# Mixture-of-experts handover: routing order, first group's places, a store's queue and the hold on expert loads

## Chip, cores and metric

The kernel runs on one core of one Trainium2 chip. The metric is device microseconds of one execution; lower is better. All inputs lie in HBM, the output is written to HBM.

## What is computed

One encoder layer over 1024 tokens of width 1024: latent attention and a two-way gated recurrence, a cross attention, and then a two-level mixture of experts. The change touches the last part and the handover into it:

```python
def hier_moe(h, w_group, b_group, w_expert, b_expert, w_gate, w_up, w_down):
    ...
    g_sel = jnp.argmax(g_logits, axis=-1)                      # one of 8 groups per token
    g_weight = jnp.take_along_axis(g_prob, g_sel[:, None], axis=-1)
    e_logits = jnp.take_along_axis(e_logits, g_sel[:, None, None], axis=1)[:, 0]
    top_logit, top_local = lax.top_k(e_logits, MOE_TOP_K)      # two of the group's 8 experts
    top_w = jax.nn.softmax(top_logit, axis=-1) * g_weight
    ...
    hb = jax.nn.silu(xb @ w_gate[e]) * (xb @ w_up[e])          # per expert, hidden width 256
    return hb @ w_down[e]
```

The result is the residual stream plus the two weighted expert outputs of each token. Each of the 64 experts has three matrices of 1 MB in float32, so 192 MB of weights are read once.

## The kernel before

**The part ahead of the change.** `cross_out(t)` (L1126 to L1157) computes the last 128 rows of tile t of the residual stream into `xt`, stores them to the scratch tensor `x3_d` (L1148) and to `out` (L1149), both on SyncE's DMA queue, and takes the mean square of each row. `logits(t)` (L1263 to L1274) turns the rows over, multiplies by the router's weights and writes 72 logits per row to `L`. This runs for t = 0 to 7; tile 7 is the last.

**Routing.** `route_groups` (L1276) handles tiles 0 to 4 early, beside the matmuls of `cross_out`, and tiles 5 to 7 at the end. It picks the group of each row, counts with triangular matmuls (`behind`) how many rows of the same group stand ahead of it, and places row numbers in `idf` by one-hot matmuls (L1334). `idx0` (L1338) holds the row numbers of group 0, in two windows of 96 rows. The inner function `route_experts` (L1340) picks two experts per row, computes weights, and the place of each row in its expert's list, into `meta`; L1377 stores it to the scratch tensor `meta_d` on ScalarE's queue.

**Handover.** `gather` (L1408) fetches a group's rows from `x3_d` into `xg0` and `xg1` by indirect DMAs on GpSimd's queue, `gather_meta` (L1418) the matching rows of `meta_d` into `mt0` and `mt1`. For group 0 both are gathered right after routing. 48 matmuls without use (L1436) run in between. The gathered `mt` also releases `idx` (L1438, the row numbers of the other groups) and, by a one-element copy on GpSimd (L1444, L1445), the loads of expert 4; the rows gathered for group 1 release those of expert 5 in the same way. Then `cnt`, `lim` and `nro` count the overflow rounds.

**Experts.** `moe` (L1602) runs 32 pairs of experts, 4 pairs per group, under an order written out by hand for TensorE, VectorE and ScalarE. For group 0 it first makes the one-hot places `gm` from `mt` (L1478), splits the rows into a high and a low part (`hi` on ScalarE, L137; `lo` on VectorE, L138), spreads them by one-hot matmuls (L1519, L1520) into `xT`, and makes the slot weights (L1498). Then per pair: `up` (L1542), `scatter` of the pair before (L1580), `turn_hidden`, a piece of the next `spread`, `down` (L1566). Gate and up matrices have 6 buffers and down matrices 4, so the loads of experts 6 and 7 are issued (L1446, L1447 on SyncE's queue) when `up` of the first pair has read experts 0 and 1, and so on; the loads of experts 4 and 5 are the last that need no expert's buffer back.

**Pools.** SBUF space is a stack. The pools `e2`, `e1` (which holds `xt`) and `ew` (which holds the cross attention's output weights) are closed before `wp2` (experts 3 to 5) and then `mx` (`xg`, `mt`) are opened on their space; `mp` (`gm`, `hi`, `lo`, `xT`) reaches over the space of the routing pool `rp`. Outside the parts with an order by hand, a scheduler orders each engine's and queue's instructions by when it takes them to be ready.

## Time and profile before

| | us |
|---|---|
| median of 3 runs | 1623.76 |
| lowest and highest of them | 1619.84, 1625.01 |
| the profiled execution's own time | 1627.78 |
| its span, first to last instruction | 1625.9 |
| PE busy | 1536.2 |
| DVE busy | 811.5 |
| ACT busy | 671.0 |
| POOL busy | 369.9 |

PE is TensorE's matmuls, PEld its weight loads, DVE VectorE, ACT ScalarE, POOL GpSimd, SP SyncE; a name with a q behind it is the engine's own sequencer or DMA issue. Times are microseconds from the span's start. A row of a timeline gives the start, the duration, the engine, the line and operation, what is written and read, the count of merged instructions, and in square brackets the idle time of the engine just before and what it waited for. The granted clock is a share of TensorE's full speed: 1.00 is 2.4 GHz and 0.50 is 1.2 GHz.

### The profile page before, as it was taken

Reading aid. Unit: us, or ns where it says so; the run is one execution under the profiler, and the core shown is the slowest. Engines: PE = TensorE matmul, PEld = TensorE weight load, DVE = VectorE, ACT = ScalarE, POOL = GpSimd, SP = SyncE. Lnnn points to the kernel's source line nnn. Section 1 sums busy time; section 2 is a strip of 40 time slices with the busy share of each in tenths; the row PEclk is TensorE's granted clock in tenths of the full one; section 3 lists DMA queues with packets and bytes.
Section 4 is the critical chain, followed back from the end, with each engine's and each line's share of the span. In section 5 each row is a group of like instructions: output and inputs, shape, how many; then the busy total and the mean of one; then the engine's idle time right before and its main releaser. Section 6 shows DMA issues by size and latency. Waiting matters only on the chain.

```text
span 1625.9 us, 25727 instructions
## 1 busy us (share of the span) xinstructions
PE 1536.2 (94%) x9956; PEld 1175.0 (72%) x9956; DVE 811.5 (50%) x1501; ACT 671.0 (41%) x1290; POOL 369.9 (23%) x497
## 2 busy tenths in 40 slices
PE   6999999998989999999999999988999999999995
PEld 6999977877878888888899988875444545444541
DVE  6177267677748777775624342253343332332321
ACT  5255234545647776664445552113232221222210
POOL 3087100000216765443122112013010110000000
PEclk9999999999999999999999999999999999999998
DMA  8144312204544553424633258978999999999992
GB/s 266 35 151 183 111 40 53 79 20 143 177 154 124 163 167 91 126 69 136 218 117 102 75 203 281 329 266 324 422 405 423 402 399 424 404 403 423 424 424 78
DMA packets 170830, 359.10 MB, mean 221 GB/s; under 512 B 31440, under 2 KB 118156, under 8 KB 146124
## 3 DMA queue, kind: packets, MB, share of 16 engines
q1 hardware_dynamic: 163504, 342.89, 57.2%
q0 software_dynamic: 4608, 14.33, 2.6%
q8 instruction: 81, 1.33, 0.3%
q10 hardware_dynamic: 2588, 0.16, 0.1%
q14 instruction: 49, 0.40, 0.1%
HBM read 296.92 MB, written 60.41 MB: 220 GB/s over the span
## 4 chain that ended last, share of the span: by engine, by line
PE 54%; issue 31%; DMA 6%; POOL 3%; DVE 3%; ACT 2%; SPq 0%; POOLq 0%; ACTq 0%; DVEq 0%
PE big L519 8%; PE sm L130 6%; PE big L1142 5%; PE sm L986 5%; PE big L167 4%; PE big L464 4%; PE big L895 3%; PE sm L895 2%; DMA out_dram<-xg,idx 2%; PE sm L553 2%; PE sm L241 2%; PE sm L738 2%; PE sm L739 2%; PE sm L826 1%; PE big L1059 1%
## 5 line engine op out<-in xcount | busy, mean ns | idle before, releaser
L1542 PE MATMUL pm<-wgu,xT 128*64 128x512 f32 x1024 | 232.3, 592 | 0.0
L1542 PEld LDWEIGHTS pm<-wgu,xT 128*64 128x64 f32 x1024 | 79.5, 137 | 142.1 <-issue 138.1
L1566 PE MATMUL pm<-wd,hT 128*64 128x512 f32 x512 | 129.8, 615 | 9.5 <-DMA wd<-in_moe_w_down_dram 7.4
L141 DVE SCALAR_TENSOR_TENSOR yl<-pm,ws,yh 128x512 fp32r<-128x512 f32 x64 | 48.0, 751 | 114.3 <-ACT yh L140 114.3
L1590 POOL DMA_INDIRECT out_dram<-xg,idx x16 | 15.1, 946 | 382.2 <-DVE xg L1588 379.8
L1566 PEld LDWEIGHTS pm<-wd,hT 128*64 128x64 f32 x512 | 37.9, 140 | 76.7 <-issue 53.5
L138 DVE TENSOR_TENSOR ptl<-sm,pth 128x512 fp32r<-128x512 f32 x128 | 84.2, 682 | 17.5 <-ACT pth L137 17.0
L137 ACT ACTIVATE pth<-sm 128x512 fp32r<-128x512 f32 x128 | 73.3, 595 | 44.0 <-PE sm L130 43.1
L140 ACT ACTIVATE yh<-pm,ws 128x512 fp32r<-128x512 f32 x64 | 44.0, 687 | 110.6 <-PE pm L1566 109.6
L725 DVE TENSOR_REDUCE st<-big 128x1 f32<-128x1024 f32 x64 | 77.9, 1217 | 15.7 <-PE big L167 12.7
L130 PE MATMUL sm<-ident,pr 128*128 128x128 f32 x576 | 83.5, 273 | 1.1 <-DVE xt L910 0.4
L1545 ACT ACTIVATE sg<-pm,ws 128x256 f32<-128x256 f32 x32 | 15.2, 475 | 167.5 <-PE pm L1542 167.5
L1546 DVE SCALAR_TENSOR_TENSOR sg<-pm,ws,sg 128x256 f32<-128x256 f32 x32 | 15.5, 484 | 129.9 <-ACT sg L1545 127.7
L130 PEld LDWEIGHTS sm<-ident,pr 128*128 128x128 f32 x576 | 68.7, 141 | 11.8 <-POOL pr L729 0.7
L727 ACT ACTIVATE pr<-big,st 128x1024 f32<-128x1024 f32 x64 | 71.4, 1116 | 11.3 <-DVE st L725 11.0
L729 POOL TENSOR_SCALAR pr<-pr,st 128x1024 f32<-128x1024 f32 x64 | 72.1, 1127 | 5.5
L1522 ACT ACTIVATE xT<-pm,wcol 128x256 f32<-128x256 f32 x64 | 30.4, 474 | 98.9 <-PE pm L1520 98.4
L738 PE MATMUL sm<-pth,mv 128*128 128x256 f32 x256 | 65.4, 292 | 3.9 <-DVE ptl L138 3.2
L1519 PE MATMUL pm<-gm,hi 96*128 96x256 f32 x256 | 66.4, 297 | 2.7 <-ACT hi L137 2.7
L1520 PE MATMUL pm<-gm,lo 96*128 96x256 f32 x256 | 63.9, 286 | 1.6 <-DVE lo L138 1.6
L739 PE MATMUL sm<-ptl,mv 128*128 128x256 f32 x256 | 63.4, 285 | 0.0
L154 ACT ACTIVATE whi<-raw 128x1024 fp32r<-128x1024 f32 (+1 forms) x52 | 47.4, 925 | 30.6 <-DMA raw<-in_x_w_kv_dram 13.2
(452 smaller groups left out, 3782.3 us busy)
## 6 DMA issues: line engine op xcount, KB each, us to landing
wgu<-in_moe_w_gate_dram SPq DMA_DIRECT2D x64, 1024.0 KB
wgu<-in_moe_w_up_dram SPq DMA_DIRECT2D x64, 1024.0 KB, 20.3
wd<-in_moe_w_down_dram SPq DMA_DIRECT2D x64, 1024.0 KB, 20.1
x_d<-xt SPq DMA_DIRECT2D x24, 512.0 KB, 5.0
raw<-in_w_in_dram SPq DMA_DIRECT2D x20, 512.0 KB, 3.7
xt<-in_x_dram SPq DMA_DIRECT2D x16, 512.0 KB, 5.8
raw<-in_x_w_kv_dram SPq DMA_DIRECT2D x16, 512.0 KB, 5.9
xt<-x_d SPq DMA_DIRECT2D x16, 512.0 KB, 4.1
```

What stands on the lines that cost most here:

```text
L130: te.transpose(out=out_, in_=in_, identity=ident[0:in_.shape[0], 0:in_.shape[0]])
L137: s.activation(hi, ps, AF.Copy)
L138: v.tensor_tensor(lo, ps, hi.bitcast(F32), op=ALU.subtract)
L519: te.matmul(ps[:, n0:n0 + 512], lhsT=l_[:, k], rhs=r_[:, k, n0:n0 + 512], start=(k == 0 and i == 0), stop=(k == KD - 1 and i == 2))
L725: v.tensor_reduce(st[:, 1:2], sp, op=ALU.max, axis=AX.X, negate=True)
L738: te.matmul(ov, lhsT=vt[:, kt], rhs=pth[:, kt], start=(kt == 0), stop=False)
L739: te.matmul(ov, lhsT=vt[:, kt], rhs=ptl[:, kt], start=False, stop=(kt == NT - 1))
L895: te.matmul(ps[:, n * 512:n * 512 + 512], lhsT=l_[:, k], rhs=r_[:, half * K2 + k, n0:n0 + 512], start=(k == 0 and i == 0), stop=(k == K2 - ...
L986: te.matmul(ps[:, j], lhsT=l_[:, k, t * P:(t + 1) * P], rhs=r_[:, k], start=(i == 0 and k == 0), stop=(i == 2 and k == KD - 1))
L1142: te.matmul(ps[:, n0:n0 + 512], lhsT=l_, rhs=r_[:, k, n0:n0 + 512], start=(k == 0 and i == 0), stop=(k == KD - 1 and i == 2))
L1542: te.matmul(ps[64 * e:64 * e + 64], lhsT=st_["xT"][q // 2][:, k, c0:c0 + CAP], rhs=we[e][:, :, k], start=(k == 0), stop=(k == KD - 1))
L1566: te.matmul(ps[64 * e:64 * e + 64], lhsT=hT[:, c, 64 * e:64 * e + 64], rhs=we[e][:, c, ns], start=(c == 0), stop=(c == 1))
```

## The change

- The last tile's store to `x3_d` moves from SyncE's to ScalarE's queue; its store to `out` stays on SyncE's.
- From the last `logits` to the handover, TensorE and VectorE follow the order of the program text, so all of `route_groups` (up to `idx0`) comes before `route_experts`.
- The places of group 0 (`mt0`, in the long-lived pool `rt`) come from a one-hot matmul at the end of `route_experts`, one part for tiles 0 to 4 and one for tiles 5 to 7; the gather of `meta_d` for group 0 is gone. `idx` is a plain copy.
- Matmuls without use stand at six places: 8, 12, 16 and 10 within the routing and 16 behind it, each 288 columns wide, in place of 48 at once.
- Expert 4's loads wait for nothing but their buffer; expert 5's wait for group 0's second window of rows.
- The counting of the rounds moves into pair 3 of `moe`.
- For group 0, `gm` is made for 4 experts, then rows and spread one half after the other, then `gm` for the other 4 experts, the row weights and the slot weights.
- The zero rows `zr` are a quarter as wide and stored by a repeated read.

```diff
-        nc.sync.dma_start(x3_d[ts, :], xt)
+        (nc.scalar if t == NT - 1 else nc.sync).dma_start(x3_d[ts, :], xt)
         nc.sync.dma_start(out[ts, :], xt)
...
+    def warm(n):
+        ps = sm(288)
+        for _ in range(n):
+            te.matmul(ps, lhsT=ones, rhs=still, start=True, stop=True)
...
+            slf, sel, mr = r8("slf", GP), r8("sel", 2), r8("mr", 2, 17)
+            v.tensor_copy(slf, sl)
+            v.tensor_tensor(sel, hoh[:, :, 0:2], og[:, :, 0:1].to_broadcast([P, n, 2]), op=ALU.mult)
+            for c0, c1, src in ((0, 8, rk), (8, 17, mt[:, :, 8:17])):
+                v.tensor_tensor(mr[:, :, :, c0:c1], src[:, :, None, :].to_broadcast([P, n, 2, c1 - c0]),
+                                sel[:, :, :, None].to_broadcast([P, n, 2, c1 - c0]), op=ALU.mult)
+            if last:
+                warm(10)
+            ps = sm(34, GP)
+            for t in range(n):
+                te.matmul(ps, lhsT=slf[:, t], rhs=mr[:, t].rearrange("p w c -> p (w c)"), start=(t == 0), stop=(t == n - 1))
...
+                v.tensor_tensor(mt0[:, :, 0:17], ps, mpart, op=ALU.add)
+                v.tensor_scalar(mt0[:, :, 0:8], mt0[:, :, 0:8], -1.0, None, op0=ALU.add)
...
+    order = ExitStack()
+    order.enter_context(tc.manual_schedule(engines={mybir.EngineType.PE, mybir.EngineType.DVE}))
     logits(NT - 1)
...
-    for _ in range(4):
-        warm = sm(288)
-        for _ in range(12):
-            te.matmul(warm[0:GP], lhsT=sl[:, 0], rhs=sl.rearrange("p t c -> p (t c)"), start=True, stop=True)
-    gather_meta(mx, ahead[0])
-    v.tensor_scalar(idx, idf[:, :, 0:2], ahead[0][1][1][:, 23:24], None, op0=ALU.add)
+    warm(16)
+    order.close()
+    for w in range(2):
+        ahead[0][w][1] = mt0[:, w]
+    v.tensor_copy(idx, idf[:, :, 0:2])
...
-    load_gu(4, ahead[0][1][1][:, 16:17])
+    load_gu(4)
+    load_gu(5, ahead[0][1][0][:, 0:1])
     ahead.append(gather(mx, idx_of(1)))
     gather_meta(mx, ahead[1])
-    load_gu(5, ahead[1][0][0][:, 0:1])
...
-        prep_places(mp, ahead.pop(0), slot0, st0)
-        prep_rows(mp, st0, 0)
-        prep_rows(mp, st0, 1)
+        first = ahead.pop(0)
+        one_hot(mp, first, slot0, st0, 0, 4)
         for kh in range(2):
+            prep_rows(mp, st0, kh)
             for _ in spread(mp, pm, st0, 0, kh):
                 pass
+        one_hot(mp, first, slot0, st0, 4, 8)
+        row_weights(mp, first, st0)
         slot_weights(mp, pm, st0)
```

## Rows read from the trace of the kernel before

**Rows 1.** The page's list of 40 equal slices of the span (40.6 us each): the mean busy share of the 16 DMA engines, in tenths.

```profile
DMA  8144312204544553424633258978999999999992
```

**Rows 2.** Busy time by stretch around and after the handover. Columns: the stretch and its length, then busy us (and instructions) of PE, PEld, DVE, ACT, POOL, the granted clock, the DMA engines' busy share and GB/s.

```profile
1078.00:1091.00 13.00, 7.18 (x70) 6.42 (x69) 9.27 (x59) 3.25 (x7) 0.55 (x1) 0.85 0.96 328
1091.00:1095.00 4.00, 4.00 (x23) 3.56 (x22) 1.59 (x10) 0.00 (x0) 1.68 (x2) 0.64 0.13 19
1095.00:1099.00 4.00, 3.14 (x26) 2.86 (x24) 0.00 (x0) 0.77 (x1) 2.44 (x3) 1.00 0.65 194
...
1113.00:1116.00 3.00, 3.00 (x18) 1.00 (x16) 0.00 (x0) 0.00 (x0) 1.61 (x4) 1.00 0.22 33
1116.00:1126.00 10.00, 10.00 (x60) 5.10 (x58) 3.28 (x6) 3.56 (x7) 0.00 (x0) 1.00 0.97 401
1126.00:1226.00 100.00, 100.00 (x524) 48.90 (x522) 37.37 (x72) 27.22 (x43) 8.27 (x8) 1.00 1.01 415
...
1526.00:1590.00 64.00, 62.11 (x306) 29.71 (x306) 18.65 (x34) 13.57 (x23) 1.86 (x2) 1.00 1.01 421
```

**Rows 3.** Who waited for whom from 1080 us on: on SyncE's DMA queue first, then on TensorE. Columns: the waiting engine and line, what it waited for, us in total, times, longest us.

```profile
SPq L1446 <- DMA wd<-in_moe_w_down_dram: 45.2, 22, 2.6
...
PEld pm L1566 <- DMA wd<-in_moe_w_down_dram: 13.1, 8, 3.4
```

**Rows 4.** Timeline of SyncE's DMA issues around the handover: expert 3's three loads, the last tile's two stores, then the loads of experts 5 and 6.

```profile
1077.89 0.33 SPq L1198 DMA_DIRECT2D wgu<-in_moe_w_gate_dram  x1
...
1078.75 0.42 SPq L1198 DMA_DIRECT2D wd<-in_moe_w_down_dram  x1
1079.27 0.60 SPq L1148 DMA_DIRECT2D x_d<-xt  x1
1079.91 0.45 SPq L1149 DMA_DIRECT2D out_dram<-xt  x1
...
1114.83 0.33 SPq L1446 DMA_DIRECT2D wgu<-in_moe_w_gate_dram  x1
...
1117.00 0.33 SPq L1446 DMA_DIRECT2D wgu<-in_moe_w_gate_dram  x1
```

**Rows 5.** Timeline of the handover, all engines: the last logits, the row numbers of group 0, the places, the gathers, the split of the rows, the spread, the slot weights and the first `up`.

```profile
1083.08 0.29 DVE L1274 SCALAR_TENSOR_TENSOR L<-sm,meta,bb 128x72 f32<-128x72 f32 x1 [2.24 <-PE sm L1273]
...
1089.98 0.16 DVE L1338 CAST idx<-idf 96x2 int32<-96x2 f32 x1
...
1090.39 7.75 PE L1436 MATMUL sm<-sl 128*96 128x288 bf16 x48
...
1092.01 0.18 DVE L1376 TENSOR_SCALAR meta<-rk 128x24 f32<-128x24 f32 x1
...
1092.26 0.37 ACTq L1377 DMA_DIRECT2D meta_d<-meta  x1
...
1093.01 1.15 POOL L1414 DMA_INDIRECT xg<-x_d,idx  x1 [11.78 <-DVE nro L1469]
...
1098.23 4.24 ACT L137 ACTIVATE hi<-xg 96x512 fp32r<-96x512 f32 x4 [9.72 <-PE sm L1436]
1099.64 0.24 DVE L1438 TENSOR_SCALAR idx<-idf,mt 96x16 int32<-96x16 f32 x1 [6.98 <-DMA mt<-meta_d,idx]
...
1101.72 4.10 DVE L138 TENSOR_TENSOR lo<-xg,hi 96x512 fp32r<-96x512 f32 x4
...
1109.00 0.95 PE L1498 MATMUL pm<-wh,gm 96*128 96x18 f32 x8
...
1109.89 2.37 PE L1542 MATMUL pm<-wgu,xT 128*64 128x512 f32 x10
```

**Rows 6.** Timeline of VectorE in the routing: two instructions of which the second needs the first, then two of which the second does not need the one just before.

```profile
1083.41 0.18 DVE L1289 TENSOR_REDUCE gm<-L 128x3 f32<-128x24 f32 x1
1083.62 0.18 DVE L1290 TENSOR_TENSOR gc<-L,gm 128x24 f32<-128x24 f32 x1
...
1085.78 0.17 DVE L1290 TENSOR_TENSOR ac<-es,am 128x24 f32<-128x24 f32 x1
1085.87 0.17 DVE L1317 TENSOR_REDUCE pos<-pb 128x3 f32<-128x24 f32 x1
```

**Rows 7.** Busy time and granted clock in stretches of the handover, columns as in rows 2.

```profile
1087.00:1093.90 6.90, 4.84 (x30) 4.10 (x31) 5.53 (x36) 0.20 (x1) 0.89 (x1) 0.51 0.57 216
1093.90:1100.70 6.80, 4.24 (x35) 3.96 (x33) 0.99 (x3) 2.47 (x3) 3.83 (x7) 1.00 0.42 118
1100.70:1107.50 6.80, 5.02 (x20) 4.46 (x21) 5.53 (x10) 2.72 (x4) 5.58 (x5) 0.50 0.97 349
```

**Rows 8.** Timeline of TensorE in the spread: two matmuls in a row at the lower and two at the higher clock.

```profile
1104.21 0.41 PE L1519 MATMUL pm<-gm,hi 96*128 96x256 f32 x1
...
1104.42 0.41 PE L1520 MATMUL pm<-gm,lo 96*128 96x256 f32 x1
...
1108.05 0.28 PE L1519 MATMUL pm<-gm,hi 96*128 96x256 f32 x1
...
1108.17 0.28 PE L1520 MATMUL pm<-gm,lo 96*128 96x256 f32 x1
```

**Rows 9.** The DMA engines at the end of the last tile's stores, one microsecond per row, columns as in rows 2.

```profile
1090.00:1091.00 1.00, 1.00 (x12) 0.93 (x12) 0.94 (x7) 0.00 (x0) 0.00 (x0) 0.50 0.83 340
1091.00:1092.00 1.00, 1.00 (x6) 0.85 (x5) 1.00 (x6) 0.00 (x0) 0.00 (x0) 0.50 0.03 12
```

76 lines of the change are left out of this document (51 added, 25 removed).

## The prediction

> **What bounds the kernel now.** I read the list of slices first. In the last third of the span the DMA engines stand at nine tenths in every slice [rows 1], and there the experts' weights are loaded. The table of stretches shows it closely: from 1116 us to 1590 us the DMA share is 0.97 to 1.01 at 401 to 421 GB/s [rows 2]. TensorE is busy there too, so I asked who waits for whom: loads wait on SyncE's queue for earlier loads, and the `down` matmuls wait for `wd` to land [rows 3]. Both nearly fill the time, and the transfers come last. So the end of the kernel is set by two things: when the stream of loads becomes continuous, and how many bytes are still missing then.
>
> Then I read the handover, 1083 to 1117 us, where the DMA engines are far from full: 0.13 of their time in 1091 to 1095 us, 0.65 in 1095 to 1099, 0.22 in 1113 to 1116 [rows 2]. Expert 5's loads are issued at 1114.83 us and flow from 1116 us; those of expert 6 are issued at 1117.00 us, when the first `up`, begun at 1109.89 us, has ended [rows 4, 5]. From there on each load waits for a buffer.
>
> **The sum in one formula.** Before, expert 5's 2.1 MB (two loads of 1,024 KB) are the head of the stream, 2.1 MB / 415 GB/s = 5.05 us [rows 2], so the loads that wait for the first `up` begin to flow at about 1121.0 us. After the change expert 5 should have landed by then, and the stream begins 1.2 us (issue to flow, 1114.83 to 1116) behind the end U of the first `up`. The end of the kernel shifts by U + 1.2 - 1121.0 = U - 1119.8. Before, U is 1117.0. So the change may let the first `up` end 2.8 us later at no loss; it wins if U comes before 1119.8 us and loses if after. The work is to find U.
>
> **Loads not held back.** Expert 4's two loads no longer wait for the gathered places, and expert 5's wait for group 0's second window instead of group 1's first. They fill the gaps of the handover: the credit of 5.05 us, in the formula already. The price: they share the DMA engines with the gathers of groups 0 and 1. From 1091 to 1099 us the gathers had these to themselves [rows 2]. I take 0 to 1.5 us on the second window, and the worse case is a rival below.
>
> **The store on ScalarE's queue.** Before, three loads of expert 3 (3.1 MB) are issued ahead of both stores [rows 4]; the engines go quiet after 1091 us [rows 9], and the first gather starts at 1093.01 us although its row numbers are ready at 1090.14 us [rows 5]. Which store was it waiting for? `x3_d` is what it reads. But it also writes into a new pool on the space of `e1`, whose last reader is the store to `out`. That a first write into a pool waits for all users of the space is seen on `hi`: it starts at 1098.23 us, 0.09 us behind the last matmul without use (1090.39 + 7.75), from which it takes no data [rows 5]. The store to `out` is the last on SyncE's queue, so I hold the gather to it, and it stays there. The bytes are the same, so `out` lands at about 1091.3 us again: gain 0, at most 2.9 us. The cost: a DMA issue takes ScalarE 0.37 us on its queue [rows 5] or SyncE 0.60 us [rows 4], ahead of the mean square and the turned rows of the last tile, on the path to the last logits: +0.5 us.
>
> The Trainium skill (page "DMA: Bandwidth & Descriptors", section "Issuing engines are not separate DMA queues") says that DMAs issued from several engines run on the same 16 DMA engines and interleave. By that rule the move brings the `x3_d` store forward only at the expense of the loads beside it, and `out` no earlier; the sum by it is the one taken here. No row of before has two such queues busy at once.
>
> **Indices first.** VectorE's instructions stand 0.21 us apart where one needs the one before, and 0.09 us where it doesn't [rows 6]. Before, both halves of the routing are interleaved and fill each other's gaps: 1083.4 to 1092.2 us [rows 5]. In text order the row numbers take 22 instructions, about 5.7 us with two trips to TensorE: `idx0` at 1089.1 us, 1.0 us sooner. The gather doesn't start then (it waits for `out`). The rest follows alone: some 35 instructions, most dependent, 8.5 us with the exponentials on ScalarE, the second count and the two new matmul steps. `mt0` is ready at 1097.8 us, against 1092.2 us for `meta` before. Added for it: 6 instructions on VectorE (1.2 us) here; the same for tiles 0 to 4 beside `cross_out` (some 1.5 us on VectorE, 0.4 us on TensorE, price -0 to +0.4 us). Removed: two gathers of `mt` and the wait for them, which before let `idx` and `gm` begin at 1099.64 us [rows 5].
>
> **Matmuls without use.** 16 of them follow `mt0`'s matmul: 48 took 7.75 us over both clock levels [rows 5], so 16 take 1.9 to 3.8 us, and end at 1099.3 us if the clock is high. `gm` and `hi` write into a pool on the routing's space, so they start behind them: T = 1099.3 + 0.5 = 1099.8 us, say 1100. The rows themselves are there at 1097 to 1100 us, so routing and rows come level.
>
> **From T to the first `up`.** Before: 1098.23 to 1109.89 = 11.7 us, all four `hi` in a row (4.24 us), all four `lo` in a row (4.10 us), then the spread [rows 5]. After: two `hi`, two `lo`, a spread, its copies, and only then the next two `hi`, since the order is by hand on all three engines. One half is 1.1 us (`hi`) + 1.1 + 1.1 (`lo`) + 0.9 (spread) + 1.9 (copies on ScalarE and VectorE in turn) = 6.1 us, two are 12.2 less an overlap of some 0.2 us. Behind them come two half `gm` and four small instructions on VectorE, 1.3 us, and the slot weights on TensorE, 0.95 us: 14.2 us. `up` is behind the slot weights on TensorE. In all 2.5 us more than before.
>
> **The clock.** Before, it fell to 0.50 for 1100.7 to 1107.5 us, after TensorE had stood idle from 1098.14 us on, and matmuls of the spread then start 0.21 us apart, against 0.12 at 1.00 [rows 5, 7, 8]. It rose 4.7 us after the spread had begun in earnest. After the change TensorE is idle for longer stretches in these 14 us, so I expect 0.50: 32 matmuls at 0.09 more each is up to 2.6 us, and half of 4.7 us in `up` itself, 2.3 us. I take half of both, 2.4 us, and keep 0 and 4.9 as bounds.
>
> The Trainium skill (page "TensorE: Matmul & The Clock Gate", section "What's actually happening") says that the throttled state is the default and activity lifts it. By that rule the matmuls spread over the routing hold the clock there, which agrees with 1.00 in 1093.9 to 1100.7 us behind the 48 [rows 7]; with the clock held up to `up` the sum would be 2.4 us lower.
>
> **The sum.** U = 1100 + 14.2 + 7.1 + 2.4 = 1123.7 us; shift 1123.7 - 1119.8 = +3.9 us, bounds +1.5 and +6.4. The profiled execution's 1627.78 us (span 1625.9) becomes 1631.7; against the median, 4.0 us lower, 1623.8 + 3.9 = 1627.7 us. The counting of rounds in pair 3 and the zero rows cost nothing: VectorE is busy 37 of 100 us there [rows 2], and the zero rows are stored long before. If that cover failed, the count's 13 instructions would cost 2 us once.
>
> **Rivals.** (a) *The store to `out` falls behind expert 4's loads.* These wait for the same released space as expert 3's, which did pass the stores [rows 4]. Two more MB ahead of `out` are 5 to 6 us, the gather starts at 1098, rows land at 1102.5, U = 1126.3: +6.5 us, 1630.3. It decides from the moment the rows land behind 1100 us. For: rows 4. Against: SyncE's issues take 0.4 us each, so the stores may be ready before its turn. (b) *The handover gets shorter as a whole.* The routing in text order keeps the pace of before (it drops 11 counting instructions), `mt0` is ready at 1093, T is 1095, the clock holds, and the tail stays at 11.7 us: U = 1113.8, -6.0 us, 1617.8. For: the gaps in rows 2. Against: rows 6 and the split order. (c) *Nothing moves:* lost start and credit cancel, or the stores don't decide the gather at all: within 1 us, 1623.8.
>
> **Chances.** Forecast 0.48, (a) 0.26, (b) 0.14, (c) 0.12. The bound of what can be told from no change is 0.3%, 4.9 us. Of the forecast three quarters lie within, one above; of (a) one fifth within. Faster 0.14, within 0.53, slower 0.33. Range: from (b), 1618, to (a) at the lower clock, 1634.
>
> **What would show it.** `out`'s end and the first `xg` gather: level means the wait is as I read it; a gather at 1090 means it was `x3_d`. `hi` within 0.1 us of the last matmul without use. The first `up` at 1114 to 1117 us. SyncE's issues: expert 4 ahead of `out` or behind. DMA share in 1100 to 1125 us: no gap means the credit was had. A later first `up` with the same end would mean that the stream isn't what sets the end. The forecast is wrong if the routing in text order is not the 14 us that I count, or if the split order overlaps more than I see.

## The result and the profile after

The changed kernel takes 1636.05 us (median of 4 runs, 1633.75 to 1637.9), the kernel before 1623.17 beside it. The ratio is 1.0079, 95% interval 1.0062 to 1.0096: slower by 12.9 us. The prediction said 1627.7, slower by 3.9; the result lies above its range. The profiled execution of after is the one of 1633.75 us (span 1632.0).

**Where to count from.** The code up to L1145 is the same in both, yet the two profiled executions reach its end at different times. Its last matmul, from the timelines of TensorE of before and then of after:

```profile
1077.47 0.39 PE L1142 MATMUL big<-xol,ah 128*128 128x512 f32 x1
```

```profile
1071.02 0.39 PE L1142 MATMUL big<-xol,ah 128*128 128x512 f32 x1
```

In the twenty kernels profiled here, all with this part unchanged, the point lies between 1070.8 and 1078.1 us: it differs from execution to execution. So the two spans (6.1 us apart) say less than the handover, and from here on a time "at +x" is counted from this matmul. Before, the first row gather starts at +15.5, `hi` at +20.8, the first `up` at +32.4, and expert 6's loads, which mark its end U, are issued at +39.5 [rows 4, 5]. After, from the timeline of all engines:

```profile
1071.58 1.04 PE L1409 MATMUL sm<-mr,slf 128*96 128x34 f32 x10 [0.17 <-DVE mr L1403]
...
1072.85 0.36 ACTq L1149 DMA_DIRECT2D x_d<-xt  x1
...
1078.64 0.29 DVE L1289 SCALAR_TENSOR_TENSOR L<-sm,meta,bb 128x72 f32<-128x72 f32 x1 [1.49 <-PE sm L1288]
...
1089.47 1.16 POOL L1456 DMA_INDIRECT xg<-x_d,idx  x1 [13.28 <-DVE e L1387]
...
1092.62 2.13 PE L1276 MATMUL sm<-still,ones 128*128 128x288 bf16 x16
...
1093.05 0.17 DVE L1413 TENSOR_SCALAR mt<-mt 96x16 f32<-96x16 f32 x1
...
1093.38 0.37 ACTq L1417 DMA_DIRECT2D meta_d<-meta  x1
...
1096.71 0.76 DVE L1519 TENSOR_TENSOR gm<-iota,mt 96x256 fp32r<-96x256 f32 x2 [3.41 <-remote]
1096.76 2.17 ACT L137 ACTIVATE hi<-xg 96x512 fp32r<-96x512 f32 x2 [8.10 <-remote]
...
1097.53 0.33 SPq L1486 DMA_DIRECT2D wgu<-in_moe_w_gate_dram  x1
...
1103.65 2.13 ACT L137 ACTIVATE hi<-xg 96x512 fp32r<-96x512 f32 x2
1104.78 2.11 DVE L138 TENSOR_TENSOR lo<-xg,hi 96x512 fp32r<-96x512 f32 x2 [0.52 <-ACT hi L137]
...
1112.13 1.94 PE L1545 MATMUL pm<-wh,gm 96*128 96x18 f32 x8 [2.03 <-DVE wh L1528]
1114.00 9.46 PE L1589 MATMUL pm<-wgu,xT 128*64 128x512 f32 x32
...
1123.49 0.33 SPq L1486 DMA_DIRECT2D wgu<-in_moe_w_gate_dram  x1
```

Read it in steps. The last logits (`L`) start at +7.6, 2.0 later than before (+5.6): TensorE first runs the ten place matmuls of tiles 0 to 4, 1.04 us, right behind the cross output, and turns the last rows only then. The other 1.0 us is not traced to one cause here. From the end of `L` to the places `mt0` it takes 14.3 us. The gather starts at +18.5, 3.0 later than before, `hi` at +25.7, 4.9 later. Both lie at the late end of what this code does: in the seven other kernels below with this store on ScalarE and expert 4's loads free, the gather starts between +16.0 and +17.5, and in a_shift64, whose handover is the same to the letter, `hi` starts at +23.9. The first `up` starts at +43.0, 10.6 later: from `hi` to it 17.2 us against 11.7. It takes 9.46 us, and U is at +52.5: 12.9 later. From the last matmul of the cross output to the end of the span it is 548.4 us before and 561.0 after, 12.6 more, which agrees with the medians (12.9). From U to the end it is 508.9 and 508.5 us: all of the loss has arisen by U, and the stream behind it is no shorter although 2.1 MB of it were loaded early.

(The matmuls without use stand at five places, not six: 8, 12, 16 and 10 in the routing, and the 16 of the row at 1092.62 us behind it.)

The stretches show what the DMA engines (second column from the right) and the clock (third) do meanwhile; columns as in [rows 2]:

```profile
1089.00:1097.00 8.00, 4.93 (x32) 3.15 (x30) 3.50 (x19) 0.24 (x1) 6.01 (x6) 0.84 0.72 200
1097.00:1107.00 10.00, 5.71 (x20) 4.37 (x20) 5.67 (x8) 4.91 (x6) 6.41 (x9) 0.57 0.92 309
1107.00:1124.00 17.00, 14.97 (x58) 8.00 (x59) 2.84 (x12) 2.69 (x4) 0.97 (x1) 0.65 0.01 2
1124.00:1134.00 10.00, 10.00 (x60) 4.86 (x60) 3.28 (x6) 3.10 (x7) 0.00 (x0) 1.00 0.94 383
1134.00:1234.00 100.00, 100.00 (x524) 49.14 (x522) 38.92 (x84) 27.88 (x44) 9.50 (x8) 1.00 1.01 408
```

Expert 5's loads are done by 1107 us, so they are out of the way as predicted. But then the engines stand idle for 17 us, share 0.01, until `up` has read a buffer: the loss up to U is larger than what the early loads save. And in the stream that follows they are as busy as before (1.01) at 408 GB/s, where before showed 415 in its first 100 us [rows 2].

### The profile page after: what moved, and what is told of

It reads as the page before. It is cut to its first block, busy times and chain, and to the rows that moved or that the text cites. A ratio compares the mean times of both kernels' runs of the same rounds, so it can differ in the third digit from the quotient of the medians.

```text
span 1632.0 us, 25788 instructions
## 1 busy us (share of the span) xinstructions
PE 1539.0 (94%) x9986; PEld 1166.9 (72%) x9986; DVE 815.4 (50%) x1514; ACT 669.8 (41%) x1290; POOL 368.6 (23%) x495
## 4 chain that ended last, share of the span: by engine, by line
PE 66%; issue 18%; DMA 7%; DVE 4%; ACT 2%; POOL 2%; SPq 0%; another core or an unknown queue 0%; POOLq 0%; ACTq 0%; DVEq 0%
PE big L519 8%; PE pm L1589 6%; PE sm L130 6%; PE sm L986 5%; PE big L1142 5%; PE big L167 4%; PE big L464 4%; PE pm L1613 3%; PE big L895 3%; PE sm L895 3%; DMA out_dram<-xg,idx 2%; PE sm L553 2%; PE sm L241 2%; PE sm L738 2%; PE sm L739 2%
## 5 line engine op out<-in xcount | busy, mean ns | idle before, releaser
L138 DVE TENSOR_TENSOR ptl<-sm,pth 128x512 fp32r<-128x512 f32 x128 | 84.2, 682 | 18.6 <-ACT pth L137 18.2
L1613 PEld LDWEIGHTS pm<-wd,hT 128*64 128x64 f32 x512 | 36.6, 141 | 79.3 <-issue 57.3
L137 ACT ACTIVATE pth<-sm 128x512 fp32r<-128x512 f32 x128 | 73.2, 594 | 42.3 <-PE sm L130 41.4
L725 DVE TENSOR_REDUCE st<-big 128x1 f32<-128x1024 f32 x64 | 77.9, 1217 | 14.4 <-PE big L167 11.2
L1593 DVE SCALAR_TENSOR_TENSOR sg<-pm,ws,sg 128x256 f32<-128x256 f32 x32 | 15.5, 484 | 130.9 <-ACT sg L1592 130.9
L727 ACT ACTIVATE pr<-big,st 128x1024 f32<-128x1024 f32 x64 | 71.3, 1114 | 12.6 <-DVE st L725 11.1
## 6 DMA issues: line engine op xcount, KB each, us to landing
wgu<-in_moe_w_up_dram SPq DMA_DIRECT2D x64, 1024.0 KB, 21.7
```

What stands on the lines that cost most here:

```text
L137: s.activation(hi, ps, AF.Copy)
L138: v.tensor_tensor(lo, ps, hi.bitcast(F32), op=ALU.subtract)
L725: v.tensor_reduce(st[:, 1:2], sp, op=ALU.max, axis=AX.X, negate=True)
L1613: te.matmul(ps[64 * e:64 * e + 64], lhsT=hT[:, c, 64 * e:64 * e + 64], rhs=we[e][:, c, ns], start=(c == 0), stop=(c == 1))
```

## The experiments

Each kernel but the first two ran in five rounds beside the kernel before. The table gives the ratio to it with its 95% interval, and from each kernel's own profiled execution the start of `hi`, of the first `up`, and U.

| kernel | ratio | interval | `hi` | `up` | U |
|---|---|---|---|---|---|
| before | 1 | | +20.8 | +32.4 | +39.5 |
| after | 1.0079 | 1.0062 to 1.0096 | +25.7 | +43.0 | +52.5 |
| a_x3sync | 1.0089 | 1.0068 to 1.0110 | +24.6 | +41.9 | +51.8 |
| a_tail | 1.0031 | 1.0017 to 1.0045 | +26.0 | +36.4 | +43.5 |
| a_nowarm | 1.0065 | 1.0046 to 1.0084 | +23.4 | +40.6 | +50.5 |
| a_x3nowarm | 1.0077 | 1.0052 to 1.0102 | +24.6 | +42.0 | +50.9 |
| a_tail_nowarm | 1.0010 | 0.9996 to 1.0025 | +23.8 | +33.4 | +40.5 |
| a_tail_held | 1.0001 | 0.9984 to 1.0018 | +24.6 | +34.3 | +41.4 |
| a_fill | 1.0053 | 1.0036 to 1.0070 | +23.8 | +41.2 | +50.0 |
| b_loads | 1.0032 | 1.0016 to 1.0048 | +23.2 | +41.2 | +48.3 |
| b_shift | 1.0030 | 1.0018 to 1.0043 | +20.4 | +33.4 | +40.5 |
| a_shift64 | 1.0063 | 1.0049 to 1.0078 | +23.9 | +41.1 | +49.8 |
| b_right | 0.9974 | 0.9962 to 0.9986 | +21.7 | +33.4 | +40.5 |
| best_al | 0.9979 | 0.9967 to 0.9991 | +24.7 | +34.2 | +41.3 |
| b_order | 1.0039 | 1.0024 to 1.0055 | +21.1 | +39.3 | +49.0 |
| b_x3act | 1.0004 | 0.9991 to 1.0017 | +20.9 | +33.8 | +40.9 |
| best_two | 0.9981 | 0.9964 to 0.9997 | +21.0 | +34.0 | +41.1 |
| best_fill | 0.9984 | 0.9965 to 1.0003 | +21.2 | +33.8 | +40.9 |
| a_two | 1.0003 | 0.9988 to 1.0018 | +25.8 | +36.6 | +43.7 |
| a_three | 0.9989 | 0.9977 to 1.0001 | +23.3 | +34.7 | +44.6 |

Names with a_ come from the changed kernel, those with b_ from the one before; the four kernels with the handover of before (before, b_shift, b_right, b_x3act) put U at +39.5 to +40.9, so the profile of before is the early end of that. Each place is read from one execution, and places differ between executions by 1 to 3 us; the ratios are from all of them.

### The store, the order and the last matmuls, taken back one at a time

a_x3sync:

```diff
-        (nc.scalar if t == NT - 1 else nc.sync).dma_start(x3_d[ts, :], xt)
+        nc.sync.dma_start(x3_d[ts, :], xt)
```

> The changed kernel with one edit taken back: the last tile's x3 store goes out on SyncE again, behind expert 3's loads and ahead of the out store. Counted from the last matmul of the cross attention's output (line 1142), the changed kernel issues group 0's first row gather at 18.5 us (before: 15.5), starts the one-hots at 25.7 (20.7), starts the first up at 43.0 (32.4) and ends it at 52.5 (39.5). Theory A, the path has several late links one behind the other: the x3 rows landed at 17.3 us from ScalarE's queue, so the gathers move 3.0 us earlier, to about 15.5; but the one-hots start when the last warm-up matmul is done (its semaphore rose at 25.7), and that does not move, so the time falls by only 0 to 0.5 us and the ratio to the kernel before stays at 1.0076 to 1.0079. Rival B, the store's queue is what made the change slow: everything behind the gather moves with it, the time falls by 3 us and the ratio by 0.0018. Rival C, with the store ahead of it the out store and the expert loads of SyncE land later and the gather stays at 18: no change for another reason, seen in the gather's issue.

The gather moved to +15.9 as expected; the time did not fall (1.0089, the interval overlaps the change's). Rival B, that the store costs 3 us, is not what the run shows. `hi`, which theory A held at +25.7, came at +24.6. A side effect speaks for the change: with the store on SyncE ScalarE takes the last tile's mean square ahead of the turned rows of the tile before, and the last logits start at +8.3 instead of +7.6, as in each kernel here that has routing from the change and this store on SyncE.

a_tail:

```diff
-        one_hot(mp, first, slot0, st0, 0, 4)
+        one_hot(mp, first, slot0, st0)
+        row_weights(mp, first, st0)
+        prep_rows(mp, st0, 0)
+        prep_rows(mp, st0, 1)
         for kh in range(2):
-            prep_rows(mp, st0, kh)
             for _ in spread(mp, pm, st0, 0, kh):
                 pass
-        one_hot(mp, first, slot0, st0, 4, 8)
-        row_weights(mp, first, st0)
```

> The changed kernel with group 0's preparation in the order of the kernel before: whole one-hots and row weights first, both halves of the rows split next, then both spreads; the rows' places still come from the matmuls. Theory A: between the halves TensorE waits for the split of the second half, 3.9 us, and its granted clock stays at 0.50 through both spreads and half of the first up; in the old order the spreads run in one piece. From the start of the one-hots to the first up 11.7 us (the kernel before at full clock) to 15, instead of 17.3, and the first up 7.1 to 9.4 instead of 9.46: the time falls by 3 to 8 us, ratio 1.003 to 1.006. Rival D, the order is innocent: TensorE is idle from the warm-up's end to the first spread in either order, the clock falls anyway, and the old order only puts 0.8 us of one-hots and 0.6 us of row weights ahead of the split: 0 to 2 us slower or no change, ratio 1.008 to 1.009.

1.0031: 7.8 us less than the change, the top of theory A's 3 to 8. From its timeline:

```profile
1094.33 3.27 PE L1276 MATMUL sm<-still,ones 128*128 128x288 bf16 x16
...
1098.22 1.29 DVE L1519 TENSOR_TENSOR gm<-iota,mt 96x512 fp32r<-96x512 f32 x2 [3.19 <-PE sm L1276]
1098.27 4.20 ACT L137 ACTIVATE hi<-xg 96x512 fp32r<-96x512 f32 x4 [8.38 <-PE sm L1276]
...
1107.78 0.95 PE L1545 MATMUL pm<-wh,gm 96*128 96x18 f32 x8
1108.67 7.09 PE L1589 MATMUL pm<-wgu,xT 128*64 128x512 f32 x32
```

All four `hi` stand in a row, the slot weights take 0.95 us instead of 1.94, `up` 7.09 instead of 9.46. From `hi` to `up` 10.4 us. The first two rows show another link: `gm` and `hi` wait for the 16 matmuls without use.

a_nowarm takes these away, a_x3nowarm them and the store:

```diff
     route_experts()
-    warm(16)
     order.close()
```

> The changed kernel without the last 16 warm-up matmuls, those behind the places of group 0. Theory A: the one-hots start when the last of these matmuls is reported done, 25.7 us after the last cross output matmul, while the first half window's rows landed at 23.1 and the places were ready at 22.2; without them the one-hots start at 22.5 and the first split at 23.6, the clock is at 0.50 through the spreads anyway, and the time falls by 2 us, ratio 1.0067. Rival E, these matmuls hold the clock: without them it falls some 4 us earlier and comes back no earlier, the first up runs at 1.2 GHz as a whole, and what the earlier start gives is lost: no change to 2 us slower. Rival F, the one-hots wait for a transfer and not for the matmuls: the start stays at 25.7.

> Both: the last tile's x3 store back on SyncE, and the last 16 warm-up matmuls left out. Theory A: the two late links hide each other, so together they give more than the sum of both alone: the gather at 15.5, the first rows at 20, and then the one-hots start when the places are ready, 22.2 us; the time falls by 3 to 4 us, ratio 1.0055 to 1.006, though the first alone gives at most 0.5 and the second 2. Rival B: 3 us for the store plus what the matmuls cost, 5 in all. Rival E: the clock takes it back, no change.

Without them `hi` starts at +23.4, 2.3 sooner, and the ratio is 1.0065; the intervals overlap. How much of the 2.3 us is theirs varies with the execution: a_shift64 has the 16, too, and starts `hi` at +23.9, 0.1 us behind their end. Four pairs of kernels differ by these 16 alone (after and a_nowarm, a_x3sync and a_x3nowarm, a_tail and a_tail_nowarm, a_two and a_three): without them 2.3, 1.9, 3.4 and 2.3 us less, no pair clear of noise by itself, but all four the same way. So a gain of some 2 us is likely. In the change's own profile their release is a step that no row explains: the 16 end at 1092.62 + 2.13 us, and `gm` is released 2 us behind that, at 1096.71.

The larger gain of both together did not come: the gather left at +15.9, but `hi` only started at +24.6. Theory A was wrong on what is late next. From the timeline of ScalarE in a_x3nowarm:

```profile
1097.39 0.42 ACTq L1417 DMA_DIRECT2D meta_d<-meta  x1
1098.40 2.14 ACT L137 ACTIVATE hi<-xg 96x512 fp32r<-96x512 f32 x2 [6.24 <-DMA xg<-x_d,idx]
```

`hi` stands on ScalarE behind the store of `meta`, and that store waits for the end of the routing. In all seven kernels of the changed kernel's family without these 16 matmuls (a_nowarm, a_x3nowarm, a_tail_nowarm, a_tail_held, a_fill, best_al, a_three) `hi` starts 0.95 to 1.01 us behind this issue, while the gather went out anywhere from +15.9 to +17.5. So it is the routing's end, +22.0 to +23.3, that holds `hi`, though the view names the rows; whoever only speeds up the gather gains nothing. That it holds `hi` by way of this store's issue, and not by the space of the routing that `hi` writes into, is argued from ScalarE's order and not tested. In the kernel before this store went out at +14.8 [rows 5].

### Both links, the loads, and the clock

a_tail_nowarm is both diffs. a_tail_held adds to them the store on SyncE and a hold on expert 4's loads:

```diff
-    load_gu(4)
+    load_gu(4, ahead[0][1][0][:, 0:1])
```

> The changed kernel with two edits: group 0's preparation in the old order, and the last 16 warm-up matmuls left out. Alone they gave ratios of 1.0031 and 1.0065, where the whole change stood at 1.0079. In the run with the old order alone the one-hots and the first split still waited 3.2 us and more for the last warm-up matmul. Theory A, the two are links of one chain: the one-hots start at 22.9 us after the last cross output matmul, the first up at 33, its end at 39.7 as in the kernel before (39.5): ratio 1.000 to 1.0015. Rival E, without these matmuls the clock is at 0.50 through the whole preparation, not only in its first half, and the first up ends at 42 to 43: ratio 1.002 to 1.003.

> As the run before it, and besides the last tile's x3 store on SyncE and expert 4's loads held until the first half window's rows have landed; what is left of the change is the places by matmuls, and expert 5's loads right behind expert 4's. Theory A: the 2 MB of expert 4 lie between the stores and the row gathers and make the rows late (with the store on SyncE and loads free, the gather went out at 13.9 us and the split started only at 24.3); held, the rows land 5 to 6 us after the gather, near 20, the one-hots start when the places are ready, 22.3, and the loads lose nothing, since the DMA engines stand idle later anyway, until the first up ends: 0.5 to 1 us faster than the run before it, ratio 0.9995 to 1.001. Rival G, what the change gains is gained by the early loads: 3 to 5 us slower, 1.003 to 1.004.

1.0010 and 1.0001, both as theory A had it, with U at +40.5 and +41.4. Holding expert 4's loads from +2.6 to +23.9 costs nothing to be measured, so rival G (the early loads are the gain) falls as far as expert 4 goes; expert 5's stayed early. The places were ready at +23.2, not 22.3, for the last logits came 0.7 us later (the store on SyncE), and `hi` followed the routing, not the rows.

b_loads, the loads alone in the kernel before:

```diff
-    load_gu(4, ahead[0][1][1][:, 16:17])
+    load_gu(4)
+    load_gu(5, ahead[0][1][0][:, 0:1])
...
-    load_gu(5, ahead[1][0][0][:, 0:1])
```

> The kernel before with one part of the change alone: expert 4's loads go out behind the stores without a wait, expert 5's when the first half window's rows have landed, ahead of the second group's. Theory A: the rows share the DMA engines with 2 MB of loads and land 1 to 4 us later, so the first up ends at 40.5 to 43.5 us after the last cross output matmul instead of 39.5, and the 5 us of loads done early are mostly spent as idle time before that: ratio 0.9995 to 1.001. Rival G, the loads are the gain: the rows land as before, and the stream that follows is shorter by 2 to 5 us: ratio 0.997 to 0.9985.

1.0032, slower than either theory. Its timeline of GpSimd tells why, and that the edit was at fault:

```profile
1095.36 1.00 POOL L1414 DMA_INDIRECT xg<-x_d,idx  x1 [0.30 <-issue]
1101.59 0.18 POOL L1444 COPY wgu<-xg 96x1 f32<-96x1 f32 x1 [5.24 <-DMA xg<-x_d,idx]
...
1102.42 1.01 POOL L1423 DMA_INDIRECT mt<-meta_d,idx  x1 [0.53 <-issue]
```

The copy that releases expert 5's loads waits on GpSimd for the rows, and the gathers of the places, issued before without a gap behind the rows' [rows 5], now stand behind that copy, which waits 5.24 us: the first goes out at +24.3, against +18.3 before. So this kernel says nothing on the loads alone, only that a hold on GpSimd's queue holds all that is queued behind it.

a_fill keeps the new order and keeps TensorE at work:

```diff
     route_experts()
-    warm(16)
+    fill(sm(256), 48)
     order.close()
...
             for _ in spread(mp, pm, st0, 0, kh):
                 pass
+            fill(pm.tile([P, 512], F32, name="pm")[:, 0:256], (32, 16)[kh])
```

(`fill(ps, n)` issues n matmuls of 256 columns on the identity tile, read as bf16.)

> The changed kernel in its own order (half a one-hot, split, spread, split, spread, rest), with TensorE kept at work: the last 16 warm-up matmuls are replaced by 48 on a constant tile that nothing waits for, with 32 more between the two spreads and 16 behind the second. It tells apart what in the order costs. Theory C1, the clock: the spreads and the first up run at 2.4 GHz, their matmuls at half the spacing (0.107 instead of 0.21 us), so that from the start of the one-hots to the first up 14 to 15 us are needed instead of 17.3, and 7.1 instead of 9.5 for the first up; with the 2 us of the earlier start the time falls by 7 us, ratio 1.0035 to 1.004. Rival C2, the gap: the second half's split waits behind the first half's copies whatever the clock is: only the 2 us of the start, and 0 to 1 more, ratio 1.006 to 1.0067.

1.0053, between the two. The row of its stretches and three of TensorE's timeline:

```profile
1098.80:1115.90 17.10, 14.91 (x128) 13.31 (x128) 7.51 (x16) 5.34 (x8) 6.00 (x6) 1.00 0.54 176
```

```profile
1096.41 6.60 PE L1478 MATMUL sm<-ident 128*128 128x256 bf16 x48
1102.77 0.36 PE L1572 MATMUL pm<-gm,hi 96*128 96x256 f32 x1
...
1115.49 8.78 PE L1595 MATMUL pm<-wgu,xT 128*64 128x512 f32 x32
```

The clock was held at 1.00 for 17 us, yet from `hi` (+23.8) to `up` (+41.2) it took 17.4 us as in the change: the 48 end at 1103.0 us, 1.6 us behind the last `lo` that the first spread needs (1099.30 + 2.12), and stand in its way. Nor did the clock hold through `up`: the mean granted clock is 0.75 in 1116.0 to 1122.7 us, and `up` takes 8.78 us, where a_tail has 7.09. What the clock is worth in this order, and what the gap between the halves, is not separated by this run.

### The stream's rate

The expert stream ran slower in the changed kernel and in all that come from it. The change puts four more tiles into the long-lived pool `rt`, `mt0` and three that were in the routing's pool or were made later:

```diff
-    runs = [rp.tile([P, NR], F32, name=f"run{i}") for i in range(3)]
+    runs = [rp.tile([P, NR], F32, name=f"run{i}") for i in range(2)] + [rt.tile([P, NR], F32, name="run2")]
+    cnt = rt.tile([P, 4], F32, name="cnt")
+    lim = rt.tile([P, 16], F32, name="lim")
...
+    mt0 = rt.tile([GP, 2, 24], F32, name="mt0")
```

In the built programs these four (576 bytes of a partition) shift the left-side expert tiles from byte 19712, a multiple of 256, to 20288, which is no multiple of 128. The right-side ones lie 224 bytes over a multiple of 256 in both. Four kernels test it: a tile without use ahead of the expert tiles of before (b_shift, 576 bytes) or of after (a_shift64, 64 bytes), one on the right side (b_right, 224 bytes), and best_al: the changed kernel with the order, the last 16 matmuls, the store, the hold on expert 4's loads and the count of rounds put back as its expectation lists them, and with both sides at multiples of 256.

The edit of b_shift:

```diff
+    pad = rt.tile([P, 144], F32, name="pad")
+    g.memset(pad, 0.0)
     idf = rt.tile([GP, NG, NH], F32, name="idf")
```

> The kernel before with one unused tile of 576 bytes per partition put in ahead of the expert tiles of the left side, so that these start at byte 20288 of a partition, as in the changed kernel, and not at 19712; nothing else differs. In the traces the 8192-byte packets of the expert stream (1140 to 1600 us) took 317.1 ns on average in the kernel before and 317.4 in the run with the loads alone, but 320.3, 320.0, 320.1 and 320.4 in the changed kernel and three runs that come from it; by megabytes about half of the stream of the kernel before stands at 309 ns and half at 313 to 315, while in the changed kernel nearly all stands at 313 to 315. Theory H, the tiles' place: the change put four small tiles (576 bytes) ahead of them, 20288 is no multiple of 128 while 19712 is one of 256, and each packet into such a tile takes 5 ns longer: packets of 320 ns and, over some 22,500 packets on 16 engines, 4.5 us: ratio 1.0025 to 1.003. Rival I, the rate comes from the changed order of gathers, loads and scatters, or from the run: packets stay at 317 ns and the ratio at 1.000.

> The changed kernel with one unused tile of 64 bytes per partition ahead of the expert tiles of the left side, which brings their start from byte 20288 to 20352, a multiple of 128 (not of 256). Theory H: packets back to 317 ns, 4.5 us faster than the changed kernel, ratio to the kernel before 1.005. If only multiples of 256 count: no change, 1.0079. Rival I: no change, packets at 320 ns.

> The kernel before with an unused tile of 224 bytes at the end of the right side, which moves the expert tiles there (half of the stream) from bytes that are 32 over a multiple of 64 (155616 and so on) to multiples of 256. Theory H: now all packets take 309 ns instead of half of them, 317 falls to 312, and the kernel gets 4 us faster: ratio 0.997 to 0.998. Rival I: no change, 1.000.

> What the runs so far point to: the changed kernel with group 0's preparation in the old order, without the last 16 warm-up matmuls, the last x3 store on SyncE, expert 4's loads held until the first rows have landed, the count of rounds back in its old place; and the expert tiles of both sides at multiples of 256 bytes. The same without the last two stood at 1.0001. Theory H: 4.5 us for the left side and 4 for the right, ratio 0.994 to 0.996. Rival I: 0.999 to 1.001.

b_shift: 1.0030; b_right: 0.9974. Theory H gave 1.0025 to 1.003 and 0.997 to 0.998. The same stretch deep in the stream, from before, after, b_shift and b_right in turn; the last three numbers are the clock, the DMA share and GB/s:

```profile
1480.00:1580.00 100.00, 99.15 (x515) 49.26 (x515) 34.37 (x63) 24.79 (x42) 3.76 (x4) 1.00 1.01 424
```

```profile
1480.00:1580.00 100.00, 100.00 (x516) 48.43 (x513) 34.64 (x63) 24.77 (x42) 3.73 (x4) 1.00 1.01 420
```

```profile
1480.00:1580.00 100.00, 98.90 (x510) 51.06 (x510) 33.67 (x63) 24.26 (x42) 3.75 (x4) 1.00 1.01 421
```

```profile
1480.00:1580.00 100.00, 99.42 (x501) 52.18 (x497) 32.36 (x60) 22.88 (x39) 3.75 (x4) 1.00 1.01 426
```

The share is 1.01 in all four; what differs is what a busy engine moves. a_shift64 stayed at 420 GB/s: 128 is not enough. Its 1.0063 goes with an earlier U, not with the rate; by the ratio alone it would not be told from 1.005 or from the change.

The traces hold the DMA packets, too. Those of 8,192 bytes in 1140 to 1600 us took 317.1 ns on average before, 320.3 after, 320.2 in b_shift, 319.7 in a_shift64 and 314.4 in b_right, where 94% of them took 309. Each of these edits moves about half of the stream, so an estimate from the differences is 6 ns a packet for 64 bytes over a multiple of 256 (2.0%), and 5 ns (1.7%) for 128 and for 224 bytes over.

The Trainium skill (page "DMA: Bandwidth & Descriptors", section "How a descriptor splits into AXI transactions") says that a transfer is cut at addresses that are multiples of 256 bytes, and that one which starts elsewhere pays for bytes that it doesn't use. By that page's count 64, 128 and 224 bytes too many on 8,192 would be an estimated 0.8%, 1.6% and 2.7%. The traces agree on the step at 256, but not on a price that grows with the bytes: it is about the same at all three. That this split is the cause is not tested; what is shown is that the address decides.

best_al came to 0.9979 where 0.994 to 0.996 was expected: it has the rate (426 GB/s in this stretch), and yet is no faster than b_right, from which it differs by what is left of the change. Part of that may be a stretch of slower packets in its profile (last section).

### One part alone, and what is left

b_order puts the new order alone into the kernel before, the diff of a_tail the other way round.

> The kernel before with one part of the change alone: group 0's preparation in the new order (half a one-hot, split, spread, split, spread, second half of the one-hot, row weights). Theory A: the second half's split waits on ScalarE and VectorE behind the first spread's copies, some 4 to 5 us, TensorE is idle meanwhile and its clock falls; the first up starts 5 to 6 us later than in the kernel before (32.4 us after the last cross output matmul) and takes up to 2.4 us longer: 5 to 8 us slower, ratio 1.003 to 1.005. Rival J, in the changed kernel the order cost 8 us only because the rows and the clock came late there; here the warm-up of 48 matmuls lies right ahead: 0 to 2 us, ratio 1.000 to 1.001.

1.0039, 6.3 us, as theory A had it. From its timeline, and the clock by stretches:

```profile
1096.37 2.13 ACT L137 ACTIVATE hi<-xg 96x512 fp32r<-96x512 f32 x2 [10.09 <-PE sm L1436]
...
1104.17 2.15 ACT L137 ACTIVATE hi<-xg 96x512 fp32r<-96x512 f32 x2
1105.31 2.13 DVE L138 TENSOR_TENSOR lo<-xg,hi 96x512 fp32r<-96x512 f32 x2 [0.52 <-ACT hi L137]
...
1112.67 1.95 PE L1508 MATMUL pm<-wh,gm 96*128 96x18 f32 x8 [2.03 <-DVE wh L1487]
1114.55 9.63 PE L1552 MATMUL pm<-wgu,xT 128*64 128x512 f32 x32
```

```profile
1092.40:1099.20 6.80, 4.24 (x33) 3.78 (x31) 1.62 (x4) 2.13 (x2) 4.13 (x6) 1.00 0.58 138
1099.20:1119.70 20.50, 15.49 (x51) 10.32 (x53) 7.31 (x18) 5.22 (x7) 10.72 (x12) 0.50 0.81 278
```

`hi` starts where it did before (+21.1), but the second half's `hi` only 7.8 us later. From the first `hi` to `up` 18.2 us instead of 11.7, `up` 9.63, the clock at 0.50 for 20.5 us, half of `up` included. It is the picture of the change without any other part of it.

b_x3act moves only the last x3 store, as the change's first hunk does; best_two and best_fill go on from b_right:

```diff
     load_gu(4, ahead[0][1][1][:, 16:17])
+    load_gu(5, ahead[0][1][1][:, 16:17])
...
-    load_gu(5, ahead[1][0][0][:, 0:1])
```

(best_fill: 28 fill matmuls behind the 48.)

> The kernel before with one part of the change alone: the last tile's x3 store on ScalarE's queue. Theory A: its packets share the engines with expert 3's loads and come one by one, it lands 1 to 4 us later than behind those loads on SyncE (13.2 us after the last cross output matmul), and the row gather, which waits for it, goes out at 14.5 to 17 instead of 13.3 and 14.5; the places' gathers follow, and the whole end moves by 0 to 3 us: ratio 1.000 to 1.002. Rival K, as its authors would have it: the out store lands earlier with half the bytes ahead of it, the gather goes out up to 1.2 us earlier: 0.999 to 1.000.

> The kernel before with its right-side expert tiles at multiples of 256 bytes (alone 0.9974), and expert 5's loads right behind expert 4's, both held only until the places of the second half window have landed, so that no gather of group 0 stands behind them. Theory A: they fill the DMA engines up to the first up's end, the stream that follows has 2 MB less, but starts at that end, 2.8 us later than the stream started before: 5.05 less 2.8, some 2 us faster than b_right: ratio 0.996. Rival L: group 1's row gathers now stand behind 4 MB and the preparation of group 1 comes late, or the first up is no earlier: 0.997 to 0.998, nothing gained.

> best_two with 28 more matmuls on a constant tile behind the warm-up of 48, which nothing waits for: TensorE stays at work until the first spread's operands are ready. If the granted clock of the spreads (0.50 from 23.2 to 30.0 us in the kernel before) is worth something: the 64 spread matmuls run at 0.107 instead of 0.21 us, the first up starts 2 to 3 us earlier: ratio 0.994 to 0.995. If the spreads wait for the splits on ScalarE and VectorE, or the matmuls stand in their way: 0.996 to 0.998.

b_x3act: 1.0004, no change. The list of DMA issues gives the store's time from issue to landing, in the change and in b_x3act:

```profile
x_d<-xt ACTq DMA_DIRECT2D x1, 512.0 KB, 15.4
```

```profile
x_d<-xt ACTq DMA_DIRECT2D x1, 512.0 KB, 9.7
```

With expert 4's 2 MB issued behind it on the other queue, the store lands at 1072.85 + 15.4 = 1088.3 us, 1.2 us ahead of the gather; in a_shift64 and a_fill it takes 13.0 and 13.3 us, and the gather again follows by 1.2. In b_x3act, without them, it takes 9.7 us and lands 4.5 us ahead of the gather (+16.0), which so waits for something else. best_two (0.9981) and best_fill (0.9984) are no faster than b_right (0.9974): neither the early loads nor the extra matmuls give anything to be measured there.

a_two undoes both causes in the changed kernel: the old order, and the left expert tiles at byte 19968 (a multiple of 256; for room, the count of rounds and its tiles go back). a_three also leaves out the last 16 matmuls.

> The changed kernel with both causes undone: group 0's preparation in the old order, and the left expert tiles at a multiple of 256 bytes (19968), for which the count of rounds and its tiles go back to their old place and 64 bytes are put in. The old order alone stood at 1.0031. Theory A and H, the two add up: 0.0026 to 0.003 less, ratio 1.000 to 1.0007, packets in the stream at the kernel before's rate (423 to 424 GB/s in 1480 to 1580 us). If the rest of the change (store, places, warm-up, early loads) has a cost of its own: 1.001 to 1.003.

> As a_two, and without the last 16 warm-up matmuls. With the old tile places this stood at 1.0010. Theory A and H: 0.997 to 0.999, the first time that a form of the change is faster than the kernel before, because expert 5's loads are done early and the first up is no later than before. If the early loads are worth nothing: 1.000.

1.0003 and 0.9989, as theory A and H had it. The stream of a_two runs at the rate of before:

```profile
1480.00:1580.00 100.00, 99.52 (x498) 50.43 (x494) 32.05 (x60) 22.89 (x39) 3.75 (x4) 1.00 1.01 424
```

So the order and the tiles' place are all of the loss that can be measured: 1.0079 with both, 1.0003 without; alone 1.0039 and 1.0030 in the kernel before. The count of rounds moved with the tiles in a_two; from a_tail to a_two the ratio falls by 0.0028, and b_shift's tile alone costs 0.0030, so little is left for the count. The rest of the change (indices first, places by matmuls, the store, the early loads) is in sum worth nothing that can be told from no change. Two parts of it cancel in the profiles: from U to the end of the span a_two needs 503.9 us, 5.0 less than the kernel before, as fits the early loads, and its U comes 4.2 later. The last 16 matmuls have two sides: without them `hi` starts sooner, but in the old order the clock then stays at 0.50 for 17.1 us (a_three, `up` 9.9 us) and 13.7 us (a_tail_nowarm), against 6.8 in a_tail and a_two.

## Why the prediction was wrong

**What failed: the clock, T, and a term that was not there.** The sum missed by 9.0 us (12.9 against 3.9). Its U, 1123.7 us on the clock of before, is +46.2; the profile has +52.5, 6.3 later, of which T is 3.2 and the clock 3.0. From U to the end the formula wants 508.9 - 2.8 = 506.1 us; it took 508.5, 2.4 more, and that is where the slower stream shows.

The prediction's step "I take half of both, 2.4 us" should have been its upper bound and a little more: it was counted in the right place and sized at half. The granted clock of after, by stretches:

```profile
1091.50:1098.30 6.80, 2.95 (x23) 2.19 (x23) 2.02 (x10) 1.54 (x2) 4.91 (x7) 1.00 0.94 257
1098.40:1118.80 20.40, 15.13 (x51) 10.31 (x53) 7.57 (x18) 5.74 (x8) 6.76 (x6) 0.50 0.39 135
1118.80:1123.40 4.60, 4.60 (x23) 1.27 (x19) 0.00 (x0) 0.00 (x0) 0.00 (x0) 1.00 0.00 0
```

It fell to 0.50 (1.2 GHz) just as the first spread began, and stayed there through both spreads, the slot weights and the first half of `up`. In the kernel before it fell there, too, but was back at 1.00 after 6.8 us, ahead of the slot weights [rows 7]. The matmuls without use in the routing did not prevent it. From `hi` to `up` 17.2 us instead of 14.2, and `up` 9.46 instead of 7.1: 5.4 us where 2.4 stood. Of these, `up` is 2.4 and the slot weights are 1.0 (1.94 us against 0.95 at 1.00 in a_tail), which the prediction had left at the higher clock. The other 2.0 lie in the two spreads; they fit the wider spacing [rows 8], but are not shown to be the clock's alone, since a_fill took 17.4 us at 1.00 with its extra matmuls in the way. Before the fall TensorE had 2.95 busy us in 6.8. b_order shows the same 0.50 without the rest of the change.

The term that was not there is the rate of the stream. The prediction's formula takes 415 GB/s for both kernels, and no rival lets it change; the four new tiles in `rt` were in the diff and priced at nothing. b_shift measured their place: 1.0030, 4.9 us.

**The split order** was right in kind: two `hi`, a spread, its copies, then the next two, some 2.5 us at the higher clock. Alone it cost 6.3 us (b_order) and taking it back gave 7.8 (a_tail); how much of that would remain at 1.00 stays open (a_fill).

**T** was 3.2 us late. Predicted 1100 us on the clock of before, +22.5; it was +25.7 (+23.9 in a_shift64, so part of it is this execution's). The routing's length was right, 14.3 us from the last logits to `mt0` where the prediction had 14.4, but it began 2.0 us later than before: "0.4 us on TensorE, price -0 to +0.4 us" for the places of tiles 0 to 4 was wrong in its place, since these ten matmuls came on the path ahead of the last tile's turned rows (1.04 us), and "+0.5" for the store on ScalarE wrong in sign (0.7 sooner). Behind `mt0` came the matmuls without use, 3.5 us instead of 2.2. The "gain 0" of the gather was a loss of 3.0 in this execution and of 0.4 to 1.9 in the seven others with this store and these loads: there the gather follows the landing of `x3_d`, by 1.2 us in the three profiles that give it. In the kernel before, the reading that the gather does not wait for `x3_d` stands: b_x3act has it landed 4.5 us earlier. The loss cost nothing, since the rows were not what `hi` waited for.

**The formula held** to some 2 us, with single misses of 4. In b_order expert 5's loads landed before U, too, and U moves by 9.4 (+49.0 against +39.5); less 2.8 that gives +6.6, and measured is +6.3. For the change itself U at +52.5 gives 12.9 - 2.8 = +10.1, and with the rate's 4.9 us 15.0; measured 12.9. In a_three U at +44.6 would give +2.3, and it measured 1.8 faster. From U to the end of the span it is 508.9 us before, 511.5 in b_shift, 508.5 after, and 503.9 and 504.9 in a_two and a_three: that fits early loads which save 4 to 5 us there, more than the formula's 2.8, and a slower stream which in the change takes it back. Each of these is one execution.

**Rival (a)** did not happen: expert 4's loads were issued behind both stores. Something like its mechanism showed in another place: beside them the store on the other queue landed later. **Rival (b)** needed `mt0` at 1093 on the clock of before; it came at 1099.7 on it. Rival (c) fell with U. The mark "no gap in 1100 to 1125" was ill chosen: expert 5's loads were done early and the gap of 17 us came behind them, as the formula itself has it when U is late. An idle stretch ahead of U says nothing on the credit; the time from U to the end does.

## What to carry to other kernels

When a stream of DMAs is the bound, an added tile is an edit to the stream: look at where the buffers that it fills come to lie, since four small tiles cost 4.9 us here, and the reordering that one reads in the diff 6.3. Before splitting a step in two so that the first half may start earlier, look at which engine both halves share: here the second split waited behind the first half's copies, and TensorE, which fell to the lower clock in either order, had it back after 6.8 us in the kernel before and after 20.4 with the split. And a load moved ahead of a wait gains only as long as the buffer that the next load needs comes free no later; count that time, not only the gap that the load fills.

## What the runs showed of the hardware

- 8,192-byte packets took 309 ns in 94% of cases where all the expert tiles start at a multiple of 256 bytes (b_right, average 314.4); with all of them 64, 128 or 224 bytes over one (b_shift, a_shift64) mostly 312 to 321, average 319.7 to 320.2. Moving half of the stream's buffers by 224 bytes made the kernel before 0.26% faster, the largest gain of this study, by an edit that adds one unused tile.
- A 0.5 MB store on ScalarE's queue took 13.0, 13.3 and 15.4 us to land (a_shift64, a_fill, after) with 2 MB more of loads issued behind it on SyncE's queue, and 9.7 us without (b_x3act): issued later on another queue, they go with a slower store.
- In best_al and best_fill one stretch of some 40 us in the stream (1330 to 1370 and 1390 to 1430 us) ran at 342 ns a packet instead of 309, an estimated 4 us each (40 us less 309/342 of it). No other profile here shows it, and no edit explains it; it may be why best_al fell short of its expectation.
